# A gated linear scan issued in four bursts, its outputs normalised by token, and its weights split on GpSimd

## The chip, the core and the metric

The kernel runs on one core of one Trainium2 chip. Its engines work side by side, each through its own queue in order: TensorE (PE, matmuls, from SBUF into PSUM), VectorE (DVE), ScalarE (ACT), GpSimd (POOL) and SyncE (SP), which here only issues transfers. Waits between engines are semaphores. The metric is device time in microseconds (us) of one execution.

## The reference

One step of a small diffusion backbone over 640 tokens (128 context, 512 latent) of width 1024: layer 0 has a bidirectional gated linear recurrence (HGRN2) as its mixer, layer 1 a convolution module, each followed by an MLP of width 4096. Only the mixer of layer 0 is touched:

```python
proj = (h @ w_in).astype(F32)
q, v, f_f, f_b, g = jnp.split(proj, 5, axis=-1)
q = heads(jax.nn.silu(q) * (HGRN_KEY_DIM ** -0.5))
...
o_f, S_f = chunk_gla_scan(q, k_f, v, lg_f, s0[:, 0])
o_b, S_b = chunk_gla_scan(rev(q), rev(k_b), rev(v), rev(lg_b), s0[:, 1])
o = o_f + rev(o_b)
o = o * lax.rsqrt(jnp.mean(o * o, axis=-1, keepdims=True) + EPS)
o = o.reshape(B, T, D_MODEL) * g_norm.astype(F32) * jax.nn.silu(g)
out = o.astype(h.dtype) @ w_out
```

with eight heads of 128 channels; a scan step is `S_t = diag(g_t) S_{t-1} + k_t v_t^T, o_t = S_t^T q_t`. The fourth line from the end is the head norm: a mean of squares over the 128 channels of one head, for every token.

## The kernel before

**Linear work.** Activations lie with channels on the 128 partitions and the 640 tokens along the free axis, in two halves of 320. Values are kept as a high and a low part, so that a product takes three matmuls (high·high, L180; high·low weight, L183; low·high, L184). A unit is 128 output channels of one half: `half_unit` makes 8 x 3 = 24 matmuls into one PSUM tile `ps_mm`, then an evacuation follows. `linear` walks groups of units; for the heads a group is two units, so a head's linear runs q0 v0 q1 v1 ff0 fb0 ff1 fb1 (query, value, forward and backward gate; the digit is the half). After each half unit it calls `scan_slot`.

**Weights.** `fetch` brings a unit's weights two units ahead: a DMA by SP into `rw` (L158), a cast on ACT into the high part `wh` (L161), and the split into the low part `wl` (L165), `rw - wh`, one 128 x 1024 subtraction on DVE or four 128 x 256 pieces on POOL. In the stage of the heads DVE makes it. `rw` has four buffers; the rows of the modulation matrix (`wm`, L127, 512 KB each, reduced on DVE into `scr`, L128, two reductions to a row, 128 x 1024) go through the same four. One such step is issued in each slot.

**The scan of a head.** It is issued in the eight slots of the next head's linear, eleven stages spread evenly. `stage_start` makes the decays and turns v (`ps_vt`, L542). `decay` walks seven levels (1, 2, 4 ... 64 tokens): a copy of a 128 x 1280 pair on ACT into `xy` (L515), then two DVE products (L521, L523) on the gate tile `a`. `score` makes a level's 32-wide blocks of scores on PE in tiles of 32 rows (`ps_sc`, L505, 20 small matmuls to a level); the first levels are merged by masked copies on DVE, the last ones copied on ACT into `s`. `stage_kt` turns the keys, `stage_state` makes the states between tiles of 128 tokens (`ps_u`, L589; `st`, L594) and the new state that goes out, and `stage_out` makes the outputs, five tiles of 128 tokens with channels on partitions (`ps_o`, L604, L608, L609), copied by ACT into `o_all` (L610).

**The head norm.** `o_squares` squares `o_all` on ACT (L459) and sums over partitions by a matmul with `sel` into `ssq` (L461), four heads ahead of g's linear and four behind its first half. A square root and a reciprocal give `rso`; `out_head` spreads a row of it over partitions by a matmul (`ps_rb`, L683), multiplies on DVE (L685) and splits the result for the last projection. The g units 0 to 3 run while the scan of head 7 is issued, the units 4 to 7 with `out_head` between them.

The Tile scheduler sets the order of each engine's instructions from the program order and its own ranking; what is issued later may stand earlier in a queue.

## Time and profile before

| | |
|---|---|
| time, median of 3 runs | 1595.05 us (1593.73 to 1596.13) |
| the profiled execution | 1594.12 us, of which the span 1592.3 us |
| granted TensorE clock | 0.992 of full speed over the span |
| PE busy | 1572.4 us, 99% |
| DVE busy | 1127.9 us, 71% |
| ACT busy | 797.9 us, 50% |
| POOL busy | 662.3 us, 42% |
| stage of the heads and g, about | 65 to 441 us |

A busy PE is not a PE at its peak: matmuls are pipelined, their records overlap, and their ends are modelled. What a matmul costs is the distance to the next one's start. The busy share is also an average over stages; the stage that changes is a quarter of the span.

### The profile page before, as it was taken

To read this page: it belongs to the slowest core of one execution; us is meant where nothing else is said; L and a number is where in the kernel's file an instruction comes from. 1 tells how busy PE (TensorE), PEld (TensorE's weight loads), DVE (VectorE), ACT (ScalarE), POOL (GpSimd) and SP (SyncE) were. 2 spreads that over 40 slices of the span, in tenths; PEclk is the share of its full clock that TensorE was granted. 3 is DMA by queue.
4 is the path that set the end of the run, shared out by engine and by line. 5 is a ranking of instruction groups with operands and counts; after the bars stand their busy time and mean duration, and the time that the engine had idled before them with its cause. 6 is when DMAs were issued, how large, how long until landed. Compare 5 with 4: busy or idle time off the path is not lost.

```text
span 1592.3 us, 32135 instructions
## 1 busy us (share of the span) xinstructions
PE 1572.4 (99%) x12810; PEld 1532.4 (96%) x12810; DVE 1127.9 (71%) x2106; ACT 797.9 (50%) x1341; POOL 662.3 (42%) x864
## 2 busy tenths in 40 slices
PE   8999999999999999999999999999999999999997
PEld 7899999989799999999999999999999999999997
DVE  5788888888637877766678995668999465444434
ACT  3566666665446523354454345764455665434431
POOL 3100000000475784554878888888888800000000
PEclk7999999999999999999999999999999999999998
DMA  8433333332354457656544444444444435444401
GB/s 349 147 112 115 114 114 114 114 111 84 107 185 146 159 185 239 232 208 225 182 134 164 154 146 149 150 151 148 160 160 157 159 112 181 146 144 137 144 27 67
DMA packets 71302, 240.11 MB, mean 151 GB/s; under 512 B 7792, under 2 KB 14576, under 8 KB 70128
## 3 DMA queue, kind: packets, MB, share of 16 engines
q1 hardware_dynamic: 71152, 238.06, 44.7%
q8 instruction: 101, 1.65, 0.4%
q14 instruction: 49, 0.40, 0.1%
HBM read 234.36 MB, written 3.67 MB: 149 GB/s over the span
## 4 chain that ended last, share of the span: by engine, by line
PE 87%; DVE 5%; POOL 2%; ACT 2%; issue 2%; DMA 1%; SPq 0%; DVEq 0%; POOLq 0%; ACTq 0%
PE ps_mm L180 27%; PE ps_mm L184 26%; PE ps_mm L183 26%; POOL wl L165 2%; PE ps_sc L505 2%; DMA rw<-in_w_in 1%; PE ps_u L589 1%; DVE scr L128 1%; ACT xy L515 1%; PE ps_m L350 1%; DVE a L521 0%; PE ssq L461 0%; DVE a L523 0%; PE ps_o L604 0%; DVE al L280 0%
## 5 line engine op out<-in xcount | busy, mean ns | idle before, releaser
L165 POOL TENSOR_TENSOR wl<-rw,wh 128x256 fp32r<-128x256 f32 x808 | 637.2, 823 | 577.1 <-ACT wh L161 576.8
L161 ACT CAST wh<-rw 128x1024 fp32r<-128x1024 f32 x334 | 350.2, 1050 | 335.3 <-PE ps_mm L184 281.4
L180 PE MATMUL ps_mm<-bh,wh 128*128 128x320 f32 (+1 forms) x1000 | 317.6, 318 | 0.0
L184 PE MATMUL ps_mm<-bl,wh 128*128 128x320 f32 (+1 forms) x1000 | 311.6, 312 | 0.9 <-DVE bl L280 0.9
L180 PE MATMUL ps_mm<-ah,wh 128*128 128x320 f32 (+1 forms) x1000 | 310.3, 310 | 1.5 <-ACT ah L279 1.3
L183 PE MATMUL ps_mm<-bh,wl 128*128 128x320 f32 (+1 forms) x1000 | 311.6, 312 | 0.0
L183 PE MATMUL ps_mm<-ah,wl 128*128 128x320 f32 (+1 forms) x1000 | 307.4, 308 | 0.0
L184 PE MATMUL ps_mm<-al,wh 128*128 128x320 f32 (+1 forms) x1000 | 305.6, 307 | 0.0
L165 DVE TENSOR_TENSOR wl<-rw,wh 128x1024 fp32r<-128x1024 f32 x132 | 166.3, 1263 | 105.2 <-ACT wh L161 105.2
L793 DVE SCALAR_TENSOR_TENSOR ps_cv<-ub,vt,ps_cv 128x319 f32<-128x319 f32 (+1 forms) x464 | 224.1, 558 | 0.1
L180 PEld LDWEIGHTS ps_mm<-ah,wh 128*128 128x128 f32 x1000 | 187.6, 188 | 7.0 <-issue 3.1
L183 PEld LDWEIGHTS ps_mm<-ah,wl 128*128 128x128 f32 x1000 | 187.8, 188 | 3.1 <-issue 2.6
L180 PEld LDWEIGHTS ps_mm<-bh,wh 128*128 128x128 f32 x1000 | 188.0, 188 | 2.3 <-DVE cl L170 0.2
L288 DVE SCALAR_TENSOR_TENSOR xr<-ps_mm,mod,xr 128x128 f32<-128x128 f32 (+2 forms) x240 | 97.9, 435 | 130.0 <-PE ps_mm L184 129.7
L184 PEld LDWEIGHTS ps_mm<-bl,wh 128*128 128x128 f32 x1000 | 188.3, 188 | 1.3 <-DVE bl L280 1.2
L184 PEld LDWEIGHTS ps_mm<-al,wh 128*128 128x128 f32 x1000 | 187.4, 188 | 1.1 <-issue 0.5
L183 PEld LDWEIGHTS ps_mm<-bh,wl 128*128 128x128 f32 x1000 | 187.9, 188 | 0.5
L180 PE MATMUL ps_mm<-dh,wh 128*128 128x320 f32 (+1 forms) x576 | 180.8, 314 | 0.0
L184 PE MATMUL ps_mm<-dl,wh 128*128 128x320 f32 (+1 forms) x576 | 180.0, 313 | 0.0
L183 PE MATMUL ps_mm<-dh,wl 128*128 128x320 f32 (+1 forms) x576 | 179.7, 312 | 0.0
L180 PE MATMUL ps_mm<-ch,wh 128*128 128x320 f32 (+1 forms) x576 | 176.7, 307 | 0.0
L184 PE MATMUL ps_mm<-cl,wh 128*128 128x320 f32 (+1 forms) x576 | 176.5, 306 | 0.0
(205 smaller groups left out, 2451.8 us busy)
## 6 DMA issues: line engine op xcount, KB each, us to landing
rw<-in_w_mlp SPq DMA_DIRECT2D x230, 512.0 KB, 3.3
wm<-in_w_modt SPq DMA_DIRECT2D x80, 512.0 KB, 4.4
rw<-in_w_pw SPq DMA_DIRECT2D x48, 512.0 KB, 3.3
rw<-in_w_in SPq DMA_DIRECT2D x40, 512.0 KB, 3.5
wmb<-in_w_mod SPq DMA_DIRECT2D x8, 1024.0 KB, 10.6
rw<-in_w_out SPq DMA_DIRECT2D x16, 512.0 KB, 3.4
x<-in_xt SPq DMA_DIRECT2D x8, 320.0 KB, 5.9
xr<-in_xt SPq DMA_DIRECT2D x8, 320.0 KB, 6.0
```

What stands on the lines that cost most here:

```text
L128: tc.keep_in_program_order(dve.scalar_tensor_tensor(scratch, box["w"][:], 1.0, cbs[:, s], ALU.mult, ALU.mult, accum_out=raw_m[:, i, s:s + 1]))
L161: act.copy(wh[:], rw[:])
L165: eng.tensor_tensor(wl[:, k:k + step], rw[:, k:k + step], wh[:, k:k + step].bitcast(F32), ALU.subtract)
L180: first = pe.matmul(ps[:, :n], wh[:, k, :], hi[:, :n], start=k == 0, stop=False)
L183: pe.matmul(ps[:, :n], wl[:, k, :], hi[:, :n], start=False, stop=False)
L184: pe.matmul(ps[:, :n], wh[:, k, :], lo[:, :n], start=False, stop=k == KT - 1)
L288: dve.scalar_tensor_tensor(x[:, u, a:b], ps[:, a - lo:b - lo], mvec(layer, chunk, u, s), x[:, u, a:b], ALU.mult, ALU.add)
L350: pin(pe.matmul(ps[32 * g:32 * g + 32, :w], cs[:, k, :], wm[:, :n, :, k, :], start=k < 4, stop=k >= 4), k)
L505: pe.matmul(ps[r:r + w, t * w:(t + 1) * w], x[:, s0:s0 + w], y[:, t0:t0 + w], start=True, stop=True, tile_position=(0, r))
L515: act.copy(ap(xy, 0, [[2 * lv, 2 * nb], [lv, 2], [1, lv]]), ap(a, 0, [[2 * lv, 2 * nb], [2 * NT + lv, 2], [1, lv]]))
L589: pe.matmul(ps[:, i * P:(i + 1) * P], hs.kt[:, 4 * d + i], hs.vt[:, t], start=True, stop=True)
L793: dve.scalar_tensor_tensor(box[i][:, :m], u[:, j:j + m], w, box[i][:, :m], ALU.mult, ALU.add)
```

## The change

Four things change together, all in the mixer of layer 0.

1. The scan of a head is issued in four bursts, at the second, fourth, sixth and eighth slot of the next head's linear, by a table of closures. Its end is carried on: states in the second slot, outputs in the fourth and their turning in the sixth of the linear after that (`old`). Levels are scored three, three and one at a time; `xy` has three buffers and the turned keys share them. For the last head all of it is packed into the slots of g's linear.
2. The outputs are made by tokens: the operands of the `ps_o` matmuls are swapped, so that 128 tokens stand on the partitions. ACT squares each tile out of PSUM with a running sum (`osq`, into `ss`), `rsqrt_small` makes the inverse root in twelve DVE operations of 128 x 5 elements, ACT scales five tiles into `ot`, five transposes on PE turn them into `ps_ot`, and two copies bring them to `o_all`. `o_squares`, `sel`, `rso` and the `ps_rb` matmuls go.
3. POOL splits the weights of units 6 to 47, in four pieces each, where DVE did.
4. The transposes of v move to the end of the head's own linear, into other PSUM tiles (`axp`), and some score tiles too; `si` has one buffer and is loaded in the fourth slot.

```diff
-            eng = pool if i in (0, 2) or 40 <= i < both_n or busy <= i < calm or (both_n <= i < busy and i % 2) else dve
+            eng = pool if i in (0, 2) or 6 <= i < both_n or busy <= i < calm or (both_n <= i < busy and i % 2) else dve
...
+    def rsqrt_small(y, m, t, scale, e):
+
+        dve.tensor_scalar(m, y, scale, e, ALU.mult, ALU.add)
+        dve.tensor_scalar(t.bitcast(I32), m.bitcast(I32), 1, None, ALU.logical_shift_right)
+        dve.tensor_scalar(y.bitcast(I32), t.bitcast(I32), -1.0, float(0x5F3759DF), ALU.mult, ALU.add)
+        for _ in range(3):
+            dve.tensor_tensor(t, y, y, ALU.mult)
+            dve.scalar_tensor_tensor(t, t, -0.5, m, ALU.mult, ALU.mult)
+            dve.scalar_tensor_tensor(y, t, 1.5, y, ALU.add, ALU.mult)
...
-    def o_squares(ssq, heads):
-        for half in range(2):
-            for i in heads:
-                sq = gp.tile([P, HALF], F32, tag="osq", name="osq", bufs=2)
-                act.activation(sq[:], o_all[:, i, half * HALF:(half + 1) * HALF], AF.Square)
-                g = i % 4
-                pe.matmul(ssq[half][32 * g:32 * g + 32, :HALF], sel[:, 32 - i // 4:64 - i // 4], sq[:],
-                          start=i < 4, stop=i >= 4)
...
-            xy = hd.tile([P, 2, NT], F32, tag="xy", name="xy", bufs=2)
+            xy = hd.tile([P, 2, NT], F32, tag="xy", name="xy", bufs=3)
...
         def stage_out(hs):
+
+            hs.ss = hd.tile([P, 3 * NTILE], F32, tag="ss", name="ss", bufs=2)
+            hs.ps_o = []
             for t0, n in PARTS:
                 ps = scp.tile([P, 512], F32, tag="sc", name="ps_o")
                 for j in range(n):
                     t = t0 + j
                     o = ps[:, j * P:(j + 1) * P]
-                    pe.matmul(o, hs.vt[:, t], hs.s[:, t], start=True, stop=t == 0)
+                    pe.matmul(o, hs.s[:, t], hs.vt[:, t], start=True, stop=t == 0)
                     if t:
                         sf = hs.si[:, 0] if t == 1 else hs.st[:, 0, t - 2]
                         sb = hs.si[:, 1] if t == 4 else hs.st[:, 1, 3 - t]
-                        pe.matmul(o, sf, hs.a[:, 3, t * P:(t + 1) * P], start=False, stop=False)
-                        pe.matmul(o, sb, hs.a[:, 1, t * P:(t + 1) * P], start=False, stop=True)
+                        pe.matmul(o, hs.a[:, 3, t * P:(t + 1) * P], sf, start=False, stop=False)
+                        pe.matmul(o, hs.a[:, 1, t * P:(t + 1) * P], sb, start=False, stop=True)
+                    junk = hd.tile([P, P], F32, tag="ns", name="osq", bufs=2)
+                    act.activation(junk[:], o, AF.Square, accum_out=hs.ss[:, t:t + 1])
+                hs.ps_o.append(ps)
+            rsqrt_small(hs.ss[:, :NTILE], hs.ss[:, NTILE:2 * NTILE], hs.ss[:, 2 * NTILE:], 1.0 / P, EPS * P)
+            hs.ot = hd.tile([P, NT], F32, tag="s", name="ot")
+            for (t0, n), ps in zip(PARTS, hs.ps_o):
+                for j in range(n):
+                    t = t0 + j
+                    act.activation(hs.ot[:, t * P:(t + 1) * P], ps[:, j * P:(j + 1) * P], AF.Copy,
+                                   scale=hs.ss[:, t:t + 1])
+
+        def stage_turn(hs):
+            for t0, n in PARTS:
+                ps = axp.tile([P, 512], F32, tag="ax", name="ps_ot")
+                for j in range(n):
+                    pe.transpose(ps[:, j * P:(j + 1) * P], hs.ot[:, (t0 + j) * P:(t0 + j + 1) * P], ident[:])
                 act.copy(o_all[:, hs.i, t0 * P:(t0 + n) * P], ps[:, :n * P])
...
+            vt = own(turn_v) if old is None else lambda: None
+            if last:
+                return {0: run(own(stage_start), dec(1, 2)), 1: end(stage_state), 2: run(own(equal), end(stage_out), own(load_state)),
+                        3: run(sc(0, 1, 2), end(stage_turn), dec(3, 4, 5)), 4: run(sc(3, 4, 5), dec(6)),
+                        5: run(sc(6), own(stage_kt)), 6: own(stage_state), 8: own(stage_out), 9: own(stage_turn)}
+            return {0: run(own(stage_start), vt, dec(1, 2)), 2: run(end(stage_state), own(equal)),
+                    4: run(end(stage_out), own(load_state), sc(0, 1, 2), dec(3, 4, 5)),
+                    6: run(end(stage_turn), sc(3, 4, 5), dec(6)),
+                    8: run(sc(6), own(stage_kt))}
...
-        o = o_all[:, i, lo:hi]
-        dve.tensor_tensor(o, ps[:, :HALF], o, ALU.mult)
-        split(o, on[half][i][0][:, :HALF], on[half][i][1][:, :HALF])
+        split(o_all[:, i, lo:hi], on[half][i][0][:, :HALF], on[half][i][1][:, :HALF])
```

Three places of the order, each in the linear of a middle head. First ACT, around the second half of q. Before, the row `sg` (evacuation of q1) is followed by a cast, a pair copy, the evacuation of v1, a pair copy and the next cast:

```order
L483 ACTIVATE sg<-ps_mm 128x320 [waits PE_49]
L161 CAST wh<-rw 128x1024 [waits DMAHW1_49]
L515 COPY xy<-a 128x1280 [waits DVE_49,PE_49,Activation_49]
L489 COPY v<-ps_mm 128x320 [waits PE_49]
L515 COPY xy<-a 128x1280 [waits DVE_49,PE_49,Activation_49]
L161 CAST wh<-rw 128x1024 [waits DMAHW3_49]
```

and in the changed kernel the same evacuation is followed by the cast, v1, and then the Squares of the outputs of the head before, with the next cast among them:

```order
L482 ACTIVATE sg<-ps_mm 128x320 [waits PE_49]
L162 CAST wh<-rw 128x1024 [waits DMAHW5_49,Pool_49]
L487 COPY v<-ps_mm 128x320 [waits PE_49]
L614 ACTIVATE osq,ss<-ps_o 128x128 [waits DMAHW6_49,PE_49]
L614 ACTIVATE osq,ss<-ps_o 128x128 [waits DMAHW7_49,PE_49,Activation_49]
L162 CAST wh<-rw 128x1024 [waits DMAHW1_49,Pool_49]
L614 ACTIVATE osq,ss<-ps_o 128x128 [waits PE_49,Activation_49]
L614 ACTIVATE osq,ss<-ps_o 128x128 [waits Activation_49]
L514 COPY xy<-a 128x1280 [waits DVE_49,PE_49]
L614 ACTIVATE osq,ss<-ps_o 128x128 [waits PE_49,Activation_49]
```

What moved: the five Squares have come to this place, and the third cast of the head's period (the one that waits for `DMAHW1`) has two of them ahead and three behind. Its fetch waits, on SP, for the low part of the second cast's unit. Before, that is a row of DVE (the first of these is the fetch, the next two the state outputs):

```order
L158 DMA rw<-in_w_in 128x1024 [waits DMAHW2_49,DVE_49]
L592 DMA out_s<-ns 128x128 [waits DMAHW5_49,Activation_49]
L592 DMA out_s<-ns 128x128 [waits Activation_49]
L127 DMA wm<-in_w_modt 128x1024 [waits DMAHW7_49,DVE_49]
L641 DMA si<-in_state 128x2x128 [waits PE_49]
```

and now one of POOL, the second `rw` row here:

```order
L592 DMA out_s<-ns 128x128 [waits Activation_49]
L592 DMA out_s<-ns 128x128 [waits DMAHW7_49,Activation_49]
L128 DMA wm<-in_w_modt 128x1024 [waits DVE_49]
L159 DMA rw<-in_w_in 128x1024 [waits DMAHW1_49,DMAHW5_49,Activation_49,Pool_49]
L128 DMA wm<-in_w_modt 128x1024 [waits DMAHW2_49,DVE_49]
```

What moved: the fetch stands behind the two state outputs and a modulation row, and its waits name ACT and POOL. Second PE, in the fourth slot's burst of the changed kernel (`ps_o` are the output tiles, each begun by an L607 row; `ps_sc` the scores of levels 0 to 2):

```order
L607 MATMUL ps_o<-vt_h,s 128x128 [waits Activation_49]
L611 MATMUL ps_o<-si,a 128x128 [waits DMAHW2_49]
L612 MATMUL ps_o<-st,a 128x128 [waits DVE_49]
L504 MATMUL ps_sc<-xy 32x32 x14
L607 MATMUL ps_o<-vt_h,s 128x128 [waits Activation_49]
L611 MATMUL ps_o<-st,a 128x128
L612 MATMUL ps_o<-st,a 128x128
L504 MATMUL ps_sc<-xy 32x32 x41
L607 MATMUL ps_o<-vt_h,s 128x128 [waits Activation_49]
L611 MATMUL ps_o<-st,a 128x128
L612 MATMUL ps_o<-si,a 128x128
L504 MATMUL ps_sc<-xy 32x32 x5
```

Before, the outputs stood alone at the end of the linear, and nothing but the copy of the finished tile read them:

```order
L184 MATMUL ps_mm<-bl,wh 128x320
L604 MATMUL ps_o<-s,vt_h 128x128 [waits PE_49,Activation_49]
L604 MATMUL ps_o<-s,vt_h 128x128
L608 MATMUL ps_o<-a,si 128x128 [waits DMAHW5_49]
L609 MATMUL ps_o<-a,st 128x128 [waits DVE_49]
```

What moved: the output tiles now stand between score blocks in the middle of the linear, and the L607 rows wait for ACT, which is the Square of the tile before in the same PSUM tile. Third DVE in the same place of the changed kernel, from the first reduction behind q1:

```order
L129 SCALAR_TENSOR_TENSOR scr,raw_m<-wm,cbs 128x1024 [waits DMAHW1_49,DVE_49]
L527 TENSOR_TENSOR tot<-tot 128x2x10
L129 SCALAR_TENSOR_TENSOR scr,raw_m<-wm,cbs 128x1024 [waits DVE_49]
L527 TENSOR_TENSOR all<-tot 128x10 [waits DVE_49]
L129 SCALAR_TENSOR_TENSOR scr,raw_m<-wm,cbs 128x1024 [waits DMAHW4_49,DVE_49]
L129 SCALAR_TENSOR_TENSOR scr,raw_m<-wm,cbs 128x1024 [waits DVE_49]
L564 COPY_PREDICATED scs<-mask,ps_sc 128x160 [waits PE_49]
L564 COPY_PREDICATED scs<-mask,ps_sc 128x160 [waits DVE_49,PE_49] x2
L520 TENSOR_TENSOR a<-a,tot 128x2x40x8 [waits Activation_49]
L248 TENSOR_SCALAR ss<-ss 128x5 [waits Activation_49]
L522 TENSOR_TENSOR a<-a,tot 128x2x40x8 [waits DVE_49]
L249 TENSOR_SCALAR ss<-ss 128x5 [waits DVE_49]
```

What moved: four reductions of modulation rows (`scr`) stand one after the other, with small products between, where the split of a weight (L165) stood among them before; and the small steps of the inverse root (`ss`) are woven into the decay products (L520, L522).

## Rows read from the trace of the kernel before

**Rows 1.** Page, part 1: busy us (share of the span) and instructions of each engine.

```profile
PE 1572.4 (99%) x12810; PEld 1532.4 (96%) x12810; DVE 1127.9 (71%) x2106; ACT 797.9 (50%) x1341; POOL 662.3 (42%) x864
```

**Rows 2.** Table by stretch: start:end, length, busy us (count) by engine, PE clock, DMA.

```profile
200.00:250.00 50.00, 50.00 (x762) 47.69 (x761) 43.98 (x82) 28.79 (x46) 0.00 (x0) 1.00 0.35 108
...
400.00:450.00 50.00, 47.81 (x283) 42.06 (x283) 30.92 (x54) 23.93 (x40) 25.10 (x28) 1.00 0.37 127
```

**Rows 3.** Timeline of PE, 249 to 255: start us, us, line, operation, count.

```profile
249.79 0.31 PE L183 MATMUL ps_mm<-ah,wl 128*128 128x320 f32 x1
...
253.01 0.31 PE L184 MATMUL ps_mm<-al,wh 128*128 128x320 f32 x1
253.25 0.56 PE L505 MATMUL ps_sc<-xy 128*32 128x32 f32 x40
...
254.00 0.31 PE L183 MATMUL ps_mm<-ah,wl 128*128 128x320 f32 x1
```

**Rows 4.** Timeline of PE, 208 to 236: bursts of scores, outputs, transposes.

```profile
208.92 0.92 PE L505 MATMUL ps_sc<-xy 128*32 128x32 f32 x80
...
229.86 0.39 PE L604 MATMUL ps_o<-s,vt_h 128*128 128x128 f32 x2
...
230.53 0.39 PE L604 MATMUL ps_o<-s,vt_h 128*128 128x128 f32 x2
...
235.40 0.71 PE L542 MATMUL ps_vt<-ident,v 128*128 128x128 f32 x5
```

**Rows 5.** Line L542 by source, 200 to 290: transposes of two heads.

```profile
L542 PE MATMUL ps_vt<-ident,v x10: 271/272/273, 235.4 to 275.6; 128*128 128x128 f32 x10
```

**Rows 6.** Tiles ssq and ps_rb, whole span; L180 by line, 351 to 441.4.

```profile
L461 PE MATMUL ssq<-osq,sel x32: 432/444/457, 351.3 to 405.0; 128*32 128x320 f32 x32
...
L683 PE MATMUL ps_rb<-rso,ident x32: 431/432/536, 406.7 to 441.4; 128*128 128x320 f32 x32
...
L180 PE MATMUL ps_mm<-bh,wh 128*128 128x320 f32 x64 | 21.4, 335 | 0.0
```

**Rows 7.** Timelines of ACT, DVE and SP near 205; page part 6, weights.

```profile
204.78 0.44 ACT L483 ACTIVATE sg<-ps_mm 128x320 f32<-128x320 f32 x1 [2.39 <-PE ps_mm L184]
205.12 1.04 ACT L161 CAST wh<-rw 128x1024 fp32r<-128x1024 f32 x1
...
206.85 1.22 DVE L165 TENSOR_TENSOR wl<-rw,wh 128x1024 fp32r<-128x1024 f32 x1
...
208.10 0.33 SPq L158 DMA_DIRECT2D rw<-in_w_in  x1
...
rw<-in_w_in SPq DMA_DIRECT2D x40, 512.0 KB, 3.5
```

**Rows 8.** Groups by line and shape, 76 to 350, ACT and DVE.

```profile
L128 DVE SCALAR_TENSOR_TENSOR scr<-wm,cbs 128x1024 f32<-128x1024 f32 x56 | 68.3, 1220 | 0.0
L515 ACT COPY xy<-a 128x1280 f32<-128x1280 f32 x49 | 67.5, 1377 | 25.8 <-DVE a L523 17.8 <-DVE a L534 3.3 <-DVE tot L524 3.3
...
L521 DVE TENSOR_TENSOR a<-a,tot 128x640 f32<-128x640 f32 x42 | 34.6, 823 | 17.3 <-ACT xy L515 17.3
...
L161 ACT CAST wh<-rw 128x1024 fp32r<-128x1024 f32 x28 | 29.2, 1044 | 3.6 <-DMA rw<-in_w_in 3.4
...
L591 ACT COPY ns<-ps_u 128x128 f32<-128x128 f32 x14 | 3.6, 267 | 4.2 <-PE ps_u L589 3.9
...
L524 DVE TENSOR_TENSOR tot<-tot 128x10 f32<-128x10 f32 x7 | 1.2, 165 | 0.0
```

**Rows 9.** Timelines of POOL: splits of weights in pieces, four to a unit.

```profile
395.25 3.89 POOL L165 TENSOR_TENSOR wl<-rw,wh 128x256 fp32r<-128x256 f32 x4 [333.02 <-ACT wh L161]
...
434.65 3.07 POOL L165 TENSOR_TENSOR wl<-rw,wh 128x256 fp32r<-128x256 f32 x4 [4.87 <-ACT wh L161]
...
562.87 10.59 POOL L165 TENSOR_TENSOR wl<-rw,wh 128x256 fp32r<-128x256 f32 x8
...
579.55 14.02 POOL L165 TENSOR_TENSOR wl<-rw,wh 128x256 fp32r<-128x256 f32 x10 [6.10 <-ACT wh L161]
```

More of the change, by code (lines that the diff above doesn't have):

```diff
@@ L496, in proj_evac, with blocks @@
             return evac
-        def blocks(x, y, evac, w=SB, other=False):
-            ps = scp.tile([P, 512], F32, tag="sc", name="ps_sc")
+        def blocks(x, y, ps, w=SB, other=False):
             for t in range(NTILE):
@@ new lines, in load_state, with stages, run, dec @@
+        def load_state(hs):
+            hs.si = hd.tile([P, 2, P], F32, tag="si", name="si")
+            sync.dma_start(hs.si[:], state[:, :, hs.i])
+        def stages(hs, old, last):
+            def run(*fs):
+                return lambda: [f() for f in fs]
+            def dec(*lis):
+                return lambda: [decay(hs, li) for li in lis]
+            def sc(*lis):
+                return lambda: scores(hs, lis)
+            def end(f):
+                return (lambda: f(old)) if old else (lambda: None)
+            def own(f):
+                return lambda: f(hs)
+            vt = own(turn_v) if old is None else lambda: None
[7 more added lines that the diff above has]
+                    8: run(sc(6), own(stage_kt))}
```

124 lines of the change are left out of this document (56 added, 68 removed).

## The prediction

> **What bounds the kernel now.** I read the busy shares first: PE is busy for 99% of the span [rows 1], so the time is PE's work plus its few gaps, and an edit counts by the PE work that it takes away or adds and by the gaps that it opens or closes. Next the table of busy time by stretch, in the stage that changes: PE 50 of 50 us while the heads are projected, with DVE near 44, ACT near 29 and POOL idle; only after 400 us does PE fall to 47.8 [rows 2]. So in the heads part there is no PE gap to win back, and DVE is a second engine near its limit. Then PE's timeline gives prices, as the distance of two starts and not as a record's duration. From 249.79 to 253.01 are 22 steps of the linear: 0.1465 us each, 3.52 us for a half unit of 24 matmuls [rows 3]. From the last matmul ahead of a burst of one score block to the second one behind it pass 0.99 us, less two steps 0.70. A double block's row lasts 0.36 longer than a single's, so of the 0.70 some 0.35 are the blocks and 0.35 the change of tile shape in and out [rows 3, 4]. Five transposes last 0.71 us, less one record's 0.27, over four steps: 0.11 each; an output tile of three matmuls takes 0.67 [rows 4, 5].
>
> **What is removed: the norm's PE work.** The stretch from the first `ssq` matmul (351.3) to the last `ps_rb` one (441.4) is 90.1 us [rows 6]. It holds 6 groups of 64 linear matmuls like the one shown, 384 x 0.1465 = 56.3, and one whole head's scan. A scan costs PE what a head's period is over its eight half units: the transposes of two heads stand at 235.4 and, the fifth of the second, at 275.6 [rows 5], so the period is 275.6 - 0.4 - 235.4 = 39.8, less 28.2 makes 11.6. Left are 90.1 - 56.3 - 11.6 = 22.2 us for the 64 `ssq` and `ps_rb` records with their shape changes and the waits around them. All of it lies on PE, so **-22.2** (bounds -20 and -24).
>
> **What is added on PE.** The turned outputs need 5 transposes in 8 heads, 40 x 0.11 = +4.4. The bursts save shape changes, but fewer than "four bursts" sounds like: in the order of the changed kernel the scheduler has put output tiles between the score blocks, and a repeating head enters scores 1 + 3 + 2 + 1 = 7 times, as often as before. Over all heads I count 51 entries for 56: -5 x 0.35 = -1.7. Outputs with swapped operands are the same number of 128 x 128 matmuls: 0. Together **+2.7**.
>
> **What is moved to POOL, and the wait it makes.** Four casts of weights fall in a head's period. The raw tiles rotate through four buffers which the modulation rows share, and in the changed order the fetch of the third cast's tile waits for POOL's split of the second cast's (before: for a DVE split of 1.22 us). The second cast cannot start before the second half of q has left PSUM. From that half unit's end I walk the chain: the evacuation starts some 0.2 later (a matmul record of 0.31 less a step), and its start to the cast's end is 0.34 + 1.04 = 1.4; the split; the issue 0.05 after it (206.85 + 1.22 = 208.07, issue 208.10); landing 3.4 to 3.5; the third cast 1.04 [rows 7]. Now comes what is new: on ACT this cast stands between the Squares of output tiles 1 and 2. Behind it wait the Squares of tiles 2 and 3, each near the 0.27 of a 128 x 128 copy out of PSUM [rows 8], and PE may not start output tile 4 before the Square of tile 3 (one PSUM tile). So tile 4 can start at 0.2 + 1.4 + 0.05 + 3.45 + 1.04 + 0.55 = 6.7 us **plus the split** after q's end. PE reaches it after half a v unit, 3.5, and what the burst has in front of it: one tile of a single matmul 0.22, three of 0.67, 2.75 score blocks 0.96, two entries into scores 0.70, together 3.9. That is 7.4. PE waits for the split's length less 0.7, and behind tile 4 stands the whole linear.
>
> How long is a split on POOL? Nothing in this stretch of before shows it. Lower bound: four pieces on a quiet chip, 3.07 us [rows 9]. With one modulation row beside it, 3.89. Where DVE runs modulation rows back to back, 8 pieces took 10.59 us and 10 took 14.02 [rows 9], which is 5.3 and 5.6 for four; that is the upper bound, stretched to 6.0 since one unit may get the worst pieces. Just this is the case here: in the changed order DVE has four modulation rows in succession (1.22 each [rows 8]) from the second evacuation of q on, where before other work and a split stood between them. I take 5.3. PE then waits 5.3 - 0.7 = 4.6 us (bounds 2.4 and 5.3). Six heads repeat this pattern: **+27.6** (14 to 32). The queues around it: SP has the two state outputs and a modulation row ahead of that fetch, but these wait for ACT copies and a DVE row that are done 2 us earlier. DVE loses four splits, 4.9 us a head, and gains 12 small operations at 0.165 to 0.2, 2.2 us [rows 8], so on DVE the change is a relief; POOL needs some 21 us of a 45 us period and has room.
>
> The Trainium skill, SBUF — State Buffer, section "SBUF: two separate sides", says that a DVE operation with two SBUF inputs and a POOL operation take their shared pair of ports in turn as an exclusive lock, each for a whole instruction. By that, three of the four pieces would wait for a full DVE row, 0.77 + 3 x (1.22 + 0.77) = 6.7 us (a piece is a quarter of 3.07), and the sum below would be 8 us higher. The rows above agree in direction; their 5.3 to 5.6 are less.
>
> **The second new wait: the turned outputs.** The transposes in the third burst need the last Square, 12 small DVE steps and five scaled ACT copies. Alone that takes 0.27 + 12 x 0.17 + 3 x 0.25 = 3.1 us, and two half units (7.1 us) cover it. But in the changed order those steps are woven into the decay chain, and the copies stand behind its third copy on ACT. From the Square of tile 3 on: three `xy` copies at 1.38 less overlap, 1.3 each, four DVE steps at 0.8 and three copies of 0.2 to 0.27 [rows 8], with three small steps between them 8.2; PE's cover from there is 0.67 + 0.45 + 7.06 = 8.2. So it is zero to 1.6, the latter if POOL stretches three or four of the DVE steps by 0.4 as it does the modulation rows. I take 0.8: **+4.8** (0 to 10).
>
> **The rest.** State matmuls wait for `kt` copies made 7 us earlier, the `st` chain has 2 to 3 us to spare, xr has until the last projection: nothing. The last head is squeezed beside g, where a cast also stands between Squares but five linear matmuls stand between output tiles, and its end has the small steps in the open: **+1** (0 to 3).
>
> **Sum.** -22.2 + 2.7 + 27.6 + 4.8 + 1 = +13.9 us. The profiled execution took 1594.12, span 1592.3 and 1.8 around it; 0.9 under the median of the runs shown, 1595.05. So span 1606.2, and against the median **1609**.
>
> **Rivals.**
> 1. *The split is quick.* If modulation rows come late (they wait for DMAs), POOL runs undisturbed: split 3.1, first wait 2.4 x 6 = 14.4, second 0.3 x 6 = 1.8, with the other terms -2.3: 1593. For it: the unit that met one row took 3.89, and the stage never had POOL at work beside it. Against: four rows in DVE's order. Below a split of 3.5 us the sum is negative.
> 2. *The gain stays.* If the third cast's tile lands in time, only small waits are left: -22.2 + 2.7 + 3 + 1 = -15.5, 1580. Against: the fetch needs that split even at its lower bound. For: ACT waited only 3.4 us for weights in 28 casts [rows 8], so the chain has been well hidden so far.
> 3. *The ports alternate fully and DVE falls behind.* Split 6.7, first wait 6.0, second 1.6 in six heads: 45.6, sum +27, 1622. It decides where the stretched DVE work also delays the states that output tiles 1 to 4 need; they have 2 to 3 us. This is the other, worse side of my forecast; rivals 1 and 2 are the faster one.
> 4. *The bursts don't come about*: already in the sum, as 51 for 56.
>
> **Chances.** Forecast (split 4.5 to 6, 1600 to 1618) 0.55; rival 1 0.25; rival 2 0.07; rival 3 0.13. A difference within 0.2% (3.2 us) is about what a measurement of this kernel can't tell from none. Faster by more: rival 2 and nearly half of rival 1, 0.18. Within: the rest of rival 1 and the edge of the forecast, 0.19. Slower: 0.63. The range leaves out rival 2 and the far part of rival 3 and reaches to a rival 1 with both waits small: 1588 to 1619.
>
> **What the profile would show.** No `ssq` and `ps_rb` rows, and a g stage shorter by over 20 us. A head's period near 45 in place of 39.8, with PE at 44 to 45 of 50 us between 150 and 350. PE waits on `ps_o` for Squares, six of 4 to 5 us, and ACT waiting on casts for the DMA of `rw`; on `ps_ot` six of up to 1.6. POOL's splits at 5 us and modulation rows at 1.4. If the `ps_o` waits are near 2, rival 1 holds; if they are missing, my walk from q's end to the cast is wrong. I am also wrong if PE waits most for `ps_u`, `ps_sc` or weights, which I cost at nothing.

## The result, and the profile after

The changed kernel took 1636.12 us (median of four, 1632.44 to 1637.23) where the kernel before took 1594.69: a ratio of 1.0255, 95% interval 1.0243 to 1.0268. The direction was forecast, the size was not: 27 us above the 1609 predicted and 17 above the range. The profiled execution took 1632.44 with a span of 1630.7, which is 38.4 more than the 1592.3 of before, where +13.9 was worked out.

First the page's line of engines and the table by stretch (columns as in [rows 2]), to be held against [rows 1, 2].

```profile
PE 1573.0 (96%) x12786; PEld 1545.7 (95%) x12786; DVE 1125.3 (69%) x2150; ACT 804.7 (49%) x1439; POOL 795.3 (49%) x998
```

```profile
150.00:200.00 50.00, 45.49 (x678) 43.82 (x671) 35.71 (x71) 29.29 (x60) 15.11 (x16) 0.93 0.29 91
200.00:250.00 50.00, 45.34 (x570) 43.71 (x569) 34.89 (x68) 28.33 (x61) 15.11 (x16) 0.93 0.29 91
```

PE is as busy as before, 1573 us, although the norm's matmuls are gone, and idle for 58 us where it was idle for 20. In the heads it stands at 45.4 of 50, as forecast (44 to 45). What was not forecast is in the last but two column: PE's granted clock is 0.93 in a stretch where it was 1.00 [rows 2].

Now the waits of PE between 60 and 480 us, the stage that changes (engine, tile, line, releaser: us in all, times, longest).

```profile
PE ps_o L607 <- ACT osq L614: 27.8, 6, 5.5
PE ps_sc L504 <- ACT xy L514: 7.1, 3, 3.1
PE ps_o L607 <- DVE st L594: 2.7, 2, 1.8
PE ps_ot L628 <- DVE scs L564: 0.7, 1, 0.7
PE ps_ot L628 <- ACT ot L621: 0.4, 1, 0.4
```

Six waits for a Square, 4.15 to 5.5 us each, are the term of +27.6 in the sum, and measured 27.8. The chain behind one of them, from the timelines of four engines near 180 us:

```profile
174.24 1.06 ACT L162 CAST wh<-rw 128x1024 fp32r<-128x1024 f32 x1
...
175.38 4.84 POOL L166 TENSOR_TENSOR wl<-rw,wh 128x256 fp32r<-128x256 f32 x4 [6.98 <-ACT wh L162]
...
180.24 0.34 SPq L159 DMA_DIRECT2D rw<-in_w_in  x1
...
184.00 1.05 ACT L162 CAST wh<-rw 128x1024 fp32r<-128x1024 f32 x1 [4.61 <-DMA rw<-in_w_in]
184.95 0.27 ACT L614 ACTIVATE osq<-ps_o 128x128 f32<-128x128 f32 x1
...
185.22 0.27 ACT L614 ACTIVATE osq<-ps_o 128x128 f32<-128x128 f32 x1
...
185.63 0.79 PE L607 MATMUL ps_o<-vt_h,s 128*128 128x128 f32 x2 [4.37 <-ACT osq L614]
```

The second cast, its split on POOL (4.84 us in each of the six heads, 5.3 taken), the fetch that was held up by it, 3.76 from issue to the third cast (3.45 taken; 3.3 to 4.9 in the six heads, which spreads the waits), and behind that cast the two Squares that output tile 4 needs: the walk of the prediction, step by step.

What follows that wait was missing in it. PE's timeline behind it, and the table in steps of 2 us:

```profile
188.26 0.47 PE L185 MATMUL ps_mm<-al,wh 128*128 128x320 f32 x1
188.52 0.47 PE L181 MATMUL ps_mm<-ah,wh 128*128 128x320 f32 x1
...
191.16 0.31 PE L184 MATMUL ps_mm<-ah,wl 128*128 128x320 f32 x1
```

```profile
182.00:184.00 2.00, 0.00 (x0) 0.00 (x0) 1.97 (x5) 0.00 (x0) 0.00 (x0) 1.00 0.98 281
...
186.00:188.00 2.00, 2.00 (x18) 1.71 (x18) 0.34 (x2) 1.09 (x3) 1.91 (x3) 0.50 0.46 166
188.00:190.00 2.00, 2.00 (x9) 2.00 (x9) 1.93 (x6) 0.39 (x1) 0.00 (x0) 0.50 0.54 168
190.00:192.00 2.00, 2.00 (x12) 2.00 (x11) 1.80 (x9) 0.87 (x1) 0.00 (x0) 0.72 0.46 160
192.00:194.00 2.00, 2.00 (x16) 2.00 (x15) 0.93 (x3) 1.02 (x2) 0.00 (x0) 1.00 0.00 0
```

Behind the wait the steps of the linear are 0.266 us apart where they were 0.1465 [rows 3]: the granted clock is 0.50, the 1.2 GHz level of PE's two (1.2 and 2.4), and it is back at 1.00 some 5 us later. The 13 steps from 187.56 to 191.16 took 3.60 us for 1.90, and the output tile and the score block ahead of them were slower too.

### The profile page after: what moved, and what is told of

It reads as the page before. It is cut to its first block, busy times and chain, and to the rows that moved or that the text cites. A ratio compares the mean times of both kernels' runs of the same rounds, so it can differ in the third digit from the quotient of the medians.

```text
span 1630.7 us, 32428 instructions
## 1 busy us (share of the span) xinstructions
PE 1573.0 (96%) x12786; PEld 1545.7 (95%) x12786; DVE 1125.3 (69%) x2150; ACT 804.7 (49%) x1439; POOL 795.3 (49%) x998
## 4 chain that ended last, share of the span: by engine, by line
PE 78%; DVE 6%; POOL 6%; ACT 5%; DMA 3%; issue 2%; SPq 0%; ACTq 0%; DVEq 0%; POOLq 0%
PE ps_mm L181 24%; PE ps_mm L185 24%; PE ps_mm L184 24%; POOL wl L166 6%; DMA rw<-in_w_in 3%; ACT xy L514 2%; ACT wh L162 1%; DVE a L520 1%; DVE scr L129 1%; DVE a L522 1%; PE ps_sc L504 1%; PE ps_f L181 1%; PE ps_o L607 1%; PE ps_f L185 0%; PE ps_m L361 0%
## 5 line engine op out<-in xcount | busy, mean ns | idle before, releaser
L166 POOL TENSOR_TENSOR wl<-rw,wh 128x256 fp32r<-128x256 f32 x944 | 769.3, 848 | 482.0 <-ACT wh L162 481.5
L184 PE MATMUL ps_mm<-ah,wl 128*128 128x320 f32 (+1 forms) x1000 | 311.4, 312 | 0.0
L185 PE MATMUL ps_mm<-al,wh 128*128 128x320 f32 (+1 forms) x1000 | 309.8, 311 | 0.0
L181 PEld LDWEIGHTS ps_mm<-ah,wh 128*128 128x128 f32 x1000 | 192.0, 192 | 3.0 <-ACT ah L290 1.9
L166 DVE TENSOR_TENSOR wl<-rw,wh 128x1024 fp32r<-128x1024 f32 x98 | 125.5, 1283 | 97.6 <-ACT wh L162 97.6
L184 PEld LDWEIGHTS ps_mm<-ah,wl 128*128 128x128 f32 x1000 | 192.2, 192 | 0.2
L185 PEld LDWEIGHTS ps_mm<-al,wh 128*128 128x128 f32 x1000 | 191.4, 192 | 0.3 <-DVE al L291 0.2
## 6 DMA issues: line engine op xcount, KB each, us to landing
wmb<-in_w_mod SPq DMA_DIRECT2D x8, 1024.0 KB, 10.4
```

Source lines behind the costliest of these rows:

```text
L166: eng.tensor_tensor(wl[:, k:k + step], rw[:, k:k + step], wh[:, k:k + step].bitcast(F32), ALU.subtract)
L181: first = pe.matmul(ps[:, :n], wh[:, k, :], hi[:, :n], start=k == 0, stop=False)
L184: pe.matmul(ps[:, :n], wl[:, k, :], hi[:, :n], start=False, stop=False)
L185: pe.matmul(ps[:, :n], wh[:, k, :], lo[:, :n], start=False, stop=k == KT - 1)
```

## The experiments

The kernel before took 1593.4 to 1593.7 us (medians) beside these runs; ratios are to it. Two measures recur: a head's period, as the distance of its first `ps_vt` transpose to the next head's (a single number is the mean of the six repeating heads, from the second head's transpose to the eighth's; of five in the kernels with the old norm, whose sixth has `ssq` matmuls in it), and "the stage", from the first matmul of the first head to the first of the output projection: 375.9 us in the kernel before, 418.0 in the changed one.

### Is it POOL's split?

**e1_dve_split**: the changed kernel, splits of the stage back on DVE (units 6 to 39; those of 40 to 47 were on POOL in the kernel before too).

```diff
-            eng = pool if i in (0, 2) or 6 <= i < both_n or busy <= i < calm or (both_n <= i < busy and i % 2) else dve
+            eng = pool if i in (0, 2) or 40 <= i < both_n or busy <= i < calm or (both_n <= i < busy and i % 2) else dve
```

> The changed kernel with the weights of units 6 to 39 split on DVE again; bursts, outputs by tokens and the norm on them stay. The scheduler then puts the third cast of a head behind the Squares. Theory (POOL's split makes the fetch late, the late cast holds the Squares, PE waits 4.4 us a head and then runs some 5 us at the half clock): six waits on ps_o and six slow stretches go, 1636 - 6 x (4.6 + 2.6) = 1593, and less if the first head's waits on scores (5.7 us) go too, down to 1585. Rival (the bursts and the turned outputs themselves make the waits, POOL's splits are only beside them): above 1620.

Measured 1584.95, 0.9945 (0.9931 to 0.996), as the theory had it. PE's waits in the stage add up to 3.4 us, PE's clock stays at 1.00 in the heads, the stage lasts 367.0. The transposes of eight heads, from first to last start, by the source view of L547, first in e1 and then in the changed kernel:

```profile
L547 PE MATMUL ps_vt<-ident,v x40: 270/273/273, 72.4 to 355.1; 128*128 128x128 f32 x40
```

```profile
L547 PE MATMUL ps_vt<-ident,v x40: 270/272/273, 70.2 to 399.2; 128*128 128x128 f32 x40
```

283 us against 329. Moving the splits costs the changed kernel 51 us, more than everything else in it brings. One reservation: with the split's engine the scheduler's order changes as well; it has put the third cast behind the Squares here.

**e4_before_pool**: the other way about, the kernel before with only the splits moved.

```diff
-            eng = pool if i in (0, 2) or 40 <= i < both_n or busy <= i < calm or (both_n <= i < busy and i % 2) else dve
+            eng = pool if i in (0, 2) or 6 <= i < both_n or busy <= i < calm or (both_n <= i < busy and i % 2) else dve
```

> The kernel before with nothing changed but that POOL splits the weights of units 6 to 39. Theory (POOL's splits cost only where PE waits soon for what stands behind a late cast, or for small DVE steps beside the pieces; the kernel before has no Squares, no inverse root and 40 us of slack in its scan): 1590 to 1600, no PE wait over 1 us in the heads. Rival (splits on POOL are slow for whatever kernel, by ports and by late fetches): 1605 or more.

Measured 1621.6, 1.0176 (1.0159 to 1.0193). The theory of that moment, that the split hurts only by the Squares behind the late cast, fell; the rival had it. The waits of PE and ACT, and one place in the timelines:

```profile
PE ps_sc L505 <- ACT xy L515: 19.0, 10, 3.6
...
ACT xy L515 <- DVE a L523: 62.3, 40, 4.8
ACT wh L161 <- DMA rw<-in_w_in: 29.9, 16, 5.4
```

```profile
226.23 1.04 ACT L161 CAST wh<-rw 128x1024 fp32r<-128x1024 f32 x1 [5.44 <-DMA rw<-in_w_in]
227.19 1.25 ACT L515 COPY xy<-a 128x1280 f32<-128x1280 f32 x1
...
228.49 0.76 PE L505 MATMUL ps_sc<-xy 128*32 128x32 f32 x40 [3.60 <-ACT xy L515]
```

The same late cast, here with the copy `xy` of the decay chain behind it, and the score blocks of PE behind that. A kernel without any Square at this place has a period of 44.0 for 39.8, and behind four of its waits (2.4 to 3.6 us) 9 to 13 steps of the linear at the 1.2 GHz level; three waits of 2.0 to 2.4 left the clock at 1.00.

### Which part of it?

**e7_second_dve**: the changed kernel, only the second split of a head on DVE.

```diff
-            eng = pool if i in (0, 2) or 6 <= i < both_n or busy <= i < calm or (both_n <= i < busy and i % 2) else dve
+            eng = pool if i in (0, 2) or 6 <= i < both_n and (i >= 40 or i % 4 != 1) or busy <= i < calm or (both_n <= i < busy and i % 2) else dve
```

> The changed kernel with only the second of each head's four units split on DVE, the three others on POOL. Theory (it is this one split that the third cast's fetch waits for): within 5 us of the kernel with all splits on DVE, so 1585 to 1598. Rival (POOL at work beside DVE slows the whole chain, each split about a quarter of it): three quarters of the loss stay, 1620 to 1628.

Measured 1615.97, 1.0138 (1.0119 to 1.0157): the wait for the Squares is gone (1.2 us in all), as it must be if that split makes it, but the third cast has also moved behind the Squares, as in e1, so this run doesn't tell the split from the order. The time missed the theory by 18 us. PE now waits for the turned outputs, `PE ps_ot L628 <- ACT ot L621: 10.4, 7, 3.5`. Why, shows DVE's timeline, with POOL's row and PE's behind it:

```profile
227.42 3.92 POOL L166 TENSOR_TENSOR wl<-rw,wh 128x256 fp32r<-128x256 f32 x4 [16.31 <-ACT wh L162]
...
227.89 0.71 DVE L248 TENSOR_SCALAR ss<-ss 128x5 f32<-128x5 f32 x1
...
228.74 0.55 DVE L249 TENSOR_SCALAR ss<-ss 128x5 int32<-128x5 int32 x1
...
229.94 0.71 DVE L250 TENSOR_SCALAR ss<-ss 128x5 int32<-128x5 int32 x1
230.69 0.66 DVE L252 TENSOR_TENSOR ss<-ss 128x5 f32<-128x5 f32 x1
231.39 0.17 DVE L253 SCALAR_TENSOR_TENSOR ss<-ss 128x5 f32<-128x5 f32 x1
...
234.02 1.36 PE L628 MATMUL ps_ot<-ident,ot 128*128 128x128 f32 x5 [1.40 <-ACT ot L621]
...
237.33 0.47 PE L184 MATMUL ps_mm<-bh,wl 128*128 128x320 f32 x1
237.60 0.47 PE L185 MATMUL ps_mm<-bl,wh 128*128 128x320 f32 x1
```

While POOL works (to 231.34), the 128x5 steps of the head norm take 0.55 to 0.71 us; then 0.17. Four of them lose 2 us, on the chain to `ps_ot`. This wait is 1.4 us and yet matmuls at 0.27 distance follow it.

The Trainium skill, SBUF — State Buffer, section "SBUF: two separate sides", says that a DVE operation and a POOL operation that take the shared pair of ports hold it in turn, each for a whole instruction. This trace agrees in kind: POOL's four pieces end at 228.58, 229.27, 230.63 and 231.33, and each of the four long steps ends 0.02 us behind one of them.

**e9_dve12**: the second and third split on DVE.

```diff
+            eng = pool if i in (0, 2) or 6 <= i < both_n and (i >= 40 or i % 4 not in (1, 2)) or busy <= i < calm or (both_n <= i < busy and i % 2) else dve
```

> The changed kernel with the second and third unit of each head split on DVE, the first and fourth on POOL. In the kernel with only the second on DVE (1616) the third unit's split on POOL ran beside the small steps of the inverse root and stretched four of them from 0.17 to 0.55-0.71 us. Theory (that split is what is left to pay): the ps_ot waits fall from 1.1-3.5 to under 0.6 us and the time to 1585-1594. Rival (any split on POOL costs its share): half of the way from 1585 to 1636, over 1603.

Measured 1599.06, 1.004 (1.0025 to 1.0055), between theory and rival: `ps_ot` still waits, 6.6 us in seven, but no matmul at half clock follows these waits. Period 42.5.

**e8_cast_behind**: the changed kernel, casts and Squares held in written order.

```diff
-            act.copy(wh[:], rw[:])
+            cast = act.copy(wh[:], rw[:])
+            if 10 <= i < 40:
+                tc.keep_in_program_order(cast)
...
-                    act.activation(junk[:], o, AF.Square, accum_out=hs.ss[:, t:t + 1])
+                    tc.keep_in_program_order(act.activation(junk[:], o, AF.Square, accum_out=hs.ss[:, t:t + 1]))
```

> The changed kernel, all splits on POOL, with casts and Squares on ACT held in the order in which they are written, so that no cast stands between the Squares. Theory (the place of the cast in ACT's queue turns a late fetch into a PE wait): the ps_o waits fall under 1 us each, no half clock, 1585 to 1600. Rival (the split's length or the ports are the price, wherever the cast stands): another wait of 3 us or more a head takes its place, above 1612.

Measured 1626.02, 1.0206 (1.0189 to 1.0223), not the 1585 to 1600 of the theory but in the rival's range. PE waits 17.3 us for `ot` and 7.7 for Squares; on ACT the Squares wait 12.2 us for the state outputs' DMA, whose tiles they share, and `xy` 43.3 us for the norm's small steps. The fixed order moved far more than the cast, so this run only says that late work on ACT finds another way to PE.

**e5_late_squares**: the changed kernel, Squares after the last output tile; no output tile waits for one.

```diff
-                    junk = hd.tile([P, P], F32, tag="ns", name="osq", bufs=2)
-                    act.activation(junk[:], o, AF.Square, accum_out=hs.ss[:, t:t + 1])
...
+            for (t0, n), ps in zip(PARTS, hs.ps_o):
+                for j in range(n):
+                    junk = hd.tile([P, P], F32, tag="ns", name="osq", bufs=2)
+                    act.activation(junk[:], ps[:, j * P:(j + 1) * P], AF.Square, accum_out=hs.ss[:, t0 + j:t0 + j + 1])
```

> The changed kernel, all splits on POOL, with the Squares of a head made after all its output tiles, so that no output tile waits for a Square. The third cast still stands between the Squares. Theory (the late cast is the price, whoever waits for what stands behind it): the wait moves from ps_o to ps_ot, 2 to 4.5 us a head there, 1615 to 1636. Rival (it was the wait of an output tile for the Square of the tile before that turned the late cast into a loss): no wait over 1 us, 1585 to 1600.

Measured 1625.26, 1.02 (1.0178 to 1.0223), as the theory had it: the wait for Squares becomes the next one,

```profile
PE ps_ot L630 <- ACT ot L623: 27.0, 7, 5.2
```

27.0 us for 27.8. What stands behind the late cast differs from kernel to kernel (Squares, `xy`, `ot`); the cast is late in all of them.

### The fetch, and DVE beside POOL

**e12_after_raw5**: a fifth raw buffer, so that no fetch of a head's weights waits for a split of that head. Room is made by a bf16 junk tile and one buffer fewer for `sg` and `gs`.

```diff
-    raw = ctx.enter_context(tc.tile_pool(name="raw", bufs=4))
+    raw = ctx.enter_context(tc.tile_pool(name="raw", bufs=5))
...
-        g = gbox[0].tile([P, HALF], F32, tag="sg", name="gs", bufs=2)
+        g = gbox[0].tile([P, HALF], F32, tag="sg", name="gs", bufs=1)
...
-                    sg = hd.tile([P, HALF], F32, tag="sg", name="sg", bufs=2)
+                    sg = hd.tile([P, HALF], F32, tag="sg", name="sg", bufs=1)
...
-                                  wmp.tile([P, D], F32, name="scr")[:], 0, 1,
+                                  wmp.tile([P, D], mybir.dt.bfloat16, name="scr")[:], 0, 1,
```

> The changed kernel with a fifth raw buffer and the same two savings of room. The order on ACT keeps a cast between the Squares, and all splits stay on POOL, but in the built program no fetch of the heads waits for a split any more, only for earlier modulation rows. Theory (late fetch): the six waits of 4 to 5.5 us on ps_o fall under 1 us and with them the half clock; what is left is the inverse root beside POOL's pieces, 1 to 1.5 us a head on ps_ot as in the kernel with the second unit on DVE: 1592 to 1606. Rival (contention of POOL and DVE is the main price): 1618 or more.

Measured 1602.09, 1.0053 (1.0036 to 1.0069), a time as the theory had it, though the waits for Squares are 1.1 to 1.5 us each and not under 1. With all splits still on POOL, 34 of the 51 us between the changed kernel and e1 are back. The waits of ACT's casts for their fetch, first in the changed kernel and then here, and PE's waits here:

```profile
ACT wh L162 <- DMA rw<-in_w_in: 49.3, 16, 7.6
```

```profile
ACT wh L162 <- DMA rw<-in_w_in: 8.5, 6, 1.7
...
PE ps_o L607 <- ACT osq L614: 7.2, 6, 1.5
PE ps_ot L628 <- ACT ot L621: 5.9, 8, 1.0
PE ps_sc L504 <- ACT xy L514: 5.3, 3, 2.4
```

```profile
200.00:250.00 50.00, 47.91 (x604) 45.88 (x603) 43.12 (x75) 32.00 (x65) 26.59 (x22) 1.00 0.34 112
```

In the repeating heads the waits that are left are short, PE's clock stays at 1.00, and the period is 43.1, for 41.25 in e1 and 47.7 in the changed kernel. So 1.8 us a head of waits beyond e1's cost 1.9 here; in the changed kernel 4.4 beyond e1's cost 6.5. The first head still waits 2.4 and 2.3 us for `xy` and drops to half clock; it is 6.2 longer than e1's.

**e13_before_raw5**: the control, the kernel before with the fifth buffer and its savings (the first, third and fourth edit above).

```diff
-    raw = ctx.enter_context(tc.tile_pool(name="raw", bufs=4))
+    raw = ctx.enter_context(tc.tile_pool(name="raw", bufs=5))
...
-                                  wmp.tile([P, D], F32, name="scr")[:], 0, 1,
+                                  wmp.tile([P, D], mybir.dt.bfloat16, name="scr")[:], 0, 1,
```

> Control: the kernel before, splits on DVE as they were, with the fifth raw buffer, the 16-bit junk and the single sigmoid buffer. Every theory expects no change, since PE has no waits in the heads: 1590 to 1597. If it is faster or slower by over 5 us, the two runs with a fifth buffer have to be read against it.

Measured 1592.22, 0.9987 (0.9977 to 0.9996): the buffer by itself is worth next to nothing.

**e11_before_pool_raw5**: e13 with the splits on POOL, that is e4 without the late fetch.

```diff
+            eng = pool if i in (0, 2) or 6 <= i < both_n or busy <= i < calm or (both_n <= i < busy and i % 2) else dve
```

> The kernel before with POOL's splits (1622 with four raw buffers), and a fifth raw buffer, so that a fetch has one tile more before it must wait for a split. To make room the junk result of the modulation rows is written in 16 bits and the query's sigmoid has one buffer. In the run with four buffers a cast waited up to 5.4 us for its DMA, the pair copies of the decays stood behind it on ACT, and PE waited 2.1 to 3.6 us a head for them. Theory (POOL holds the raw tile longer, the fetch comes late, and the cast blocks ACT's queue): most of the 28 us come back, 1594 to 1604. Rival (the stretching of DVE's and POOL's operations beside each other is the price): 1612 or more.

Measured 1634.85, 1.0252 (1.0237 to 1.0268). It should have recovered as e12 did, and was 13 us slower than e4: the theory missed, the rival was right. No cast waits for a DMA here, and yet:

```profile
PE ps_sc L505 <- ACT xy L515: 28.3, 8, 4.0
...
ACT xy L515 <- DVE a L523: 85.5, 39, 5.9
```

In e13 that last wait is 6.2 us in all. DVE is late, and its steps are longer (ten of them between 210 and 236 us by 0.5 to 0.6 us each). Groups of DVE and POOL by line and shape, 76 to 350 us, in e11 and then in e13:

```profile
L128 DVE SCALAR_TENSOR_TENSOR scr<-wm,cbs 128x1024 bf16<-128x1024 f32 x48 | 65.4, 1364 | 0.0
L523 DVE TENSOR_TENSOR a<-a,tot 128x640 f32<-128x640 f32 x36 | 34.4, 955 | 0.2
...
L524 DVE TENSOR_TENSOR tot<-g 128x640 f32<-128x640 f32 x7 | 9.5, 1361 | 0.0
...
L165 POOL TENSOR_TENSOR wl<-rw,wh 128x256 fp32r<-128x256 f32 x99 | 113.9, 1182 | 160.7 <-ACT wh L161 160.7
```

```profile
L128 DVE SCALAR_TENSOR_TENSOR scr<-wm,cbs 128x1024 bf16<-128x1024 f32 x55 | 66.9, 1217 | 0.0
...
L523 DVE TENSOR_TENSOR a<-a,tot 128x640 f32<-128x640 f32 x42 | 34.4, 819 | 0.2
```

A modulation row takes 1.36 for 1.22, a decay step 0.96 for 0.82 and the first step of the chain 1.36 for 0.82, while a POOL piece takes 1.18 (0.77 alone, a quarter of 3.07 in [rows 9]). Fetches in time set the splits where the decay chain runs: of the pieces between 76 and 350 us, 61 of 98 take over 1.15 us here and 45 of 100 in e4. The move changes the order in DVE's queue too, so that the longer steps make the wait is read from the trace and not isolated by a run. On this reading the move has two prices: the late fetch, and DVE steps that get longer beside POOL. Which of them is the larger depends on what DVE does while POOL splits: in the changed kernel the fetch (34 of 51 us), in the kernel before not.

The Trainium skill, Perfetto Trace Analysis, section "Optimizing Scalar/DVE Operations", warns that moving operations between DVE and GpSimd might not help because of the port they share. e4 and e11 agree in the outcome: +28 and +41 us in a kernel in which DVE was busy for 44 of 50 us and POOL for none.

### The clock

**e3_warm**: the changed kernel with nine useless matmuls ahead of output tile 4, so that PE has work in the wait.

```diff
+                    if t == 4:
+                        warm = mmp.tile([P, 512], F32, tag="mm", name="warm")
+                        for _ in range(9):
+                            pe.matmul(warm[:, :HALF], ident[:], hs.q[:, :HALF], start=True, stop=True)
```

> The changed kernel with nine matmuls without use (fp32, 128 x 320, some 0.6 us each) ahead of output tile 4 of each head, so that PE works through the time in which it waits for the Square. Theory (waiting lowers the clock, and the half clock costs 2.6 us behind each wait): the rows at the half clock go, the waits shrink to under 1.5 us with their place filled, 1617 to 1624. Rival (the half clock has another cause, or the slow stretch costs nothing): 1634 or more.

Measured 1654.63, 1.0385 (1.0369 to 1.04). In five of six repeating heads no matmul at half clock follows, but the time expected (1617 to 1624) was missed by 31 us, into the rival's range but not for its reason: the scheduler moved all score blocks behind the added matmuls, where PE waited for the masking copies, `PE ps_sc L504 <- DVE scs L564: 10.7, 10, 1.6`, and the period grew to 49.2. So the clock's share is not measured by this run.

**e10_act_delay**: e1 with 20 further Squares behind the third output tile, to make the wait without POOL.

```diff
+                    for _ in range(20 if t == 2 else 0):
+                        act.activation(junk[:], o, AF.Square)
```

> The kernel with all splits on DVE (1585), in which the Square of output tile 2 is made 20 times more on ACT, some 0.2 us each, so that the Square of tile 3 and with it PE's output tile 4 come 3.5 to 4 us later, with POOL idle. Theory (a PE wait of this size also lowers the clock behind it, 2.2 to 2.6 us a head): rows at the half clock behind each wait, eight heads of 3.8 + 2.4, 1625 to 1635. Rival (the wait alone is paid, the half clock in the changed kernel came from something else): no slow rows, 1608 to 1617.

Measured 1593.31, 0.9999 (0.999 to 1.0008). Inconclusive: the scheduler filled the gap with score blocks, waits stayed between 0.6 and 1.74 us, and no matmul ran at half clock.

### A version that beats both

**e6_late_dve**: e1 with the late Squares of e5.

```diff
-            eng = pool if i in (0, 2) or 6 <= i < both_n or busy <= i < calm or (both_n <= i < busy and i % 2) else dve
+            eng = pool if i in (0, 2) or 40 <= i < both_n or busy <= i < calm or (both_n <= i < busy and i % 2) else dve
...
-                    act.activation(junk[:], o, AF.Square, accum_out=hs.ss[:, t:t + 1])
...
+            for (t0, n), ps in zip(PARTS, hs.ps_o):
```

> The kernel with all splits on DVE, and the Squares of a head's outputs made after all its output tiles, so that PE waits for none of them; the scheduler then sets the 60 score matmuls of that burst in one piece. Theory (entries into scores cost 0.35 us and PE's waits for Squares 0.2): two entries fewer in seven heads and no wait, 1585 - 7 x 0.9 = 1579 (1576 to 1582). Rival (the wait only moves to the turned outputs, since the Squares come later): 1584 or more, with ps_ot waits over 0.5 us.

Measured 1586.57, 0.9961 (0.9946 to 0.9976), the rival's time. The burst with output tiles and score blocks costs PE 4.3 us beyond the linear's own steps (median of the six repeating heads), where it cost 5.5 in e1, since the blocks stand together; the burst with the transposes costs 3.9 for 2.3, since `ot` is late: `PE ps_ot L630 <- ACT ot L623: 7.4, 8, 1.7`.

This run also prices the clock. Its six repeating heads have the same PE instructions in the same order, and two of them drop to half clock behind the wait. The table by stretch for one head that does and one that doesn't:

```profile
148.28:191.51 43.23, 41.87 (x554) 40.23 (x553) 34.97 (x72) 26.88 (x56) 0.00 (x0) 0.96 0.33 105
191.51:232.71 41.20, 40.59 (x554) 38.96 (x553) 34.88 (x72) 26.80 (x56) 0.00 (x0) 1.00 0.35 110
```

In the two heads with the low clock PE waits 1.72 and 1.36 us and is busy for 41.65 and 41.87; in the four others it waits 0.6 to 0.9 and is busy for 40.6. With order and POOL (idle) alike, the low clock costs 1.1 to 1.3 us a head beyond the wait.

**e15_turn7**: e6 with the transposes of the turned outputs one slot later (the seventh) and a tile of their own for `ot`.

```diff
-            hs.ot = hd.tile([P, NT], F32, tag="s", name="ot")
+            hs.ot = hd.tile([P, NT], F32, tag="ot", name="ot")
...
-                    6: run(end(stage_turn), sc(3, 4, 5), dec(6)),
+                    6: run(sc(3, 4, 5), dec(6)), 7: end(stage_turn),
```

> All splits on DVE, Squares after all output tiles, and the turning of the outputs issued one half unit later, in the seventh slot, with its own SBUF tile (room from a 16-bit junk tile). The term of the prediction that this tests: the bursts and the turned outputs should cost PE 2.7 us over all heads, but the kernel with DVE's splits spends 12.8 us a head on the scan where 12.1 were worked out. Theory (what is missing is shape changes where output and turned tiles stand among score blocks, and 0.4 us of waits): the outputs' burst at 4.5 (5.6 before), the third burst at 1.4 and the five transposes apart at 0.55 (2.4 together before), 12.8 - 1.1 - 0.45 = 11.3 us a head, 1585 - 9 = 1576 (1573 to 1580). Rival (the wait for the inverse root is the price, and a slot later it is only hidden elsewhere, by the scores behind it): 1583 or more.

Measured 1580.62 (1578.03 to 1581.65), 0.9915 (0.99 to 0.993): 0.6 us above what the theory allowed, and below the rival's bound. It is 13 us quicker than the kernel before and 55 quicker than the changed one.

```profile
L547 PE MATMUL ps_vt<-ident,v x40: 270/272/273, 74.4 to 353.3; 128*128 128x128 f32 x40
```

```profile
PE ps_sc L504 <- ACT ot L623: 5.1, 6, 1.8
```

The stage lasts 362.3 us. What is left to the theory's time is the wait for `ot` that now stands ahead of a score block.

## Why the prediction was right or wrong

The difference of the two spans, 38.4 us, taken apart with e1 as the step between: without POOL the stage is 8.9 shorter than before and the rest 0.6; with POOL the six repeating heads are 38.8 longer (47.72 each for 41.25), the first head 7.5, the end of the stage 4.6; the rest of the program is 3.1 shorter. -8.9 - 0.6 + 38.8 + 7.5 + 4.6 - 3.1 = 38.3. Beside the steps of the prediction:

| Step | Predicted us | Measured us |
|---|---|---|
| Norm off PE, and the new bursts | -22.2 + 2.7 = -19.5 | -8.9 (e1's stage) |
| Wait for a Square behind the late cast, six heads | +27.6 | +26.6 (27.8 less e1's 1.2) |
| What the six heads lose beyond these waits: the clock | not seen | +12.2 (38.8 - 26.6) |
| Wait for the turned outputs, six heads | +4.8 | 0 |
| First head, end of the stage | +1 | +12.1 |
| Rest of the program | 0 | -3.7 |

**Right: the split's chain.** Order of the two casts, the fetch behind the split, the Squares behind the cast: each link is in the trace, and 4.6 us was the mean of what PE waited. That the size came out as well is in part luck: the split was 0.46 us shorter than taken, and the fetch 0.47 longer (3.92 from issue to cast in the mean of the six, for 3.45). The six heads at 4.84 us a split lie between the rows it was taken from (3.9 and 5.3). The test of the chain is e12: the splits stay on POOL and the cast stays among the Squares, the fetch no longer waits for a split's buffer, the casts' waits fall from 49.3 to 8.5 us, and 34 us come back (the savings of room that go with it were worth nothing in e13).

**Missing: what a wait costs beyond its length.** The prediction priced 4.6 us of wait at 4.6. The heads grew by 6.5 for 4.4 more of waits than e1's: behind each of the six, 9 to 14 steps of the linear ran at the 1.2 GHz level. No row of before could show it there, since PE had no gap in the heads [rows 2]. Less their waits for Squares and turned outputs, the periods are 41.0 us in e1, 41.1 in e12 (POOL's splits, no half clock in these heads) and 43.1 here. The two runs meant to separate the clock changed the order; e6 separates it within one run, 1.1 to 1.3 us a head with the mean clock at 0.96. Here it is 0.93, so the 2.1 fit the clock, but that they are all clock isn't measured by itself.

**Mis-sized: +2.7 for the bursts.** e1's stage is 10.6 us longer than the sum's -19.5 would make it, with 3.4 of waits in that. A head's period in e1 is 41.25, with 0.3 of waits, where 39.8 and the transposes less the saved entries made 40.1. Counting entries into score blocks was not enough: output tiles and transposes stand singly among the blocks, and each change between them has its own price. e15 shows part of it is the order and not the work: with whole runs of tiles and blocks the stage is 4.7 shorter than e1's.

**Mis-sized: the ends.** The first head waits twice for `xy`, 2.64 and 3.06 us, the first time behind a cast that waited 7.6 us for its fetch, and runs at half clock after the second; at the end there are five waits of 0.4 to 1.8, 5.3 in all, 1.1 of them for the turned outputs' tiles. I put 1 us there without walking either.

**Not seen as one of two: the wait for the turned outputs.** Predicted 0.8 a head, measured none, as the wait ahead of it already gives `ot` its time. It comes as soon as the first one goes: 10.4 us in e7, 27.0 in e5, 5.9 in e12. The two terms were added though the first covers the second.

**The norm's -22.2** could not be tested by itself; e15, with the stage 13.6 us shorter than before, has it as the only term that is large enough.

**The rivals.** Rival 1, a quick split, has its answer in 4.84 us; rival 3, full alternation, is nearer in time (1622) by another mechanism than the one that acted: PE's waits at tile 4 were 4.6, not its 6.0.

## What to carry to other kernels

Before work moves to a slower engine, ask who refills the buffer that this work reads last: the refill can come later by the whole difference, and everything that stands behind its consumer in an in-order queue comes later too. Price a new wait of a busy PE above its length where the rows show a lower clock behind it, and count two waits on one chain once. An idle POOL is not free: look at what DVE runs in those microseconds, and undo the move alone before judging the rest of a change, here worth 13 us once the splits were back and the bursts in order.
